# Batched matmul on one core: single buffers for the cast weights and the transposed x, x loaded ahead, casts of x between output copies

## The chip, the cores and the metric

The kernel runs on one core of a Trainium2 chip. A core has TensorE (PE, matrix products), VectorE (DVE), ScalarE (ACT), GpSimd (POOL) and SyncE (SP), which here does nothing but issue transfers. The engines run each their own list of instructions and meet only at semaphores. Data lie in HBM (the large memory), SBUF (on chip, 128 partitions) and PSUM (where TensorE writes). The metric is the device time of one launch in microseconds (us), the median of several runs.

## The reference

```python
b1, b2, m, k, n = 8, 16, 256, 512, 384
x:      (b1, b2, m, k) float32
weight: (b1, b2, k, n) float32

def reference(x, weight):
    return np.matmul(x, weight).astype(np.float32)
```

That is 128 independent products of a 256 x 512 by a 512 x 384 matrix. 67 MB of x and 101 MB of weights are read and 50 MB of results are written.

## The kernel before

The 128 products are taken in NG = 32 groups of G = 4. The 4 x 256 rows of x of a group lie in SBUF with eight rows to a partition (R = 8), so that one partition in 32 belongs to one product (C = 32). A group is worked in T = 4 steps q of two rows each. It goes through five stages:

1. SyncE (`load`, line 97) issues two transfers of weights (1.5 MB each, for two products) into `w_sb` and one of x (2 MB) into `x_sb`. Both have buffers for two groups (XS = 2 for x, WS = 4 half groups for weights). The loads run LAG = 4 groups ahead of the stores in SyncE's list, and each waits until the buffer that it fills has been cast. `store` (line 116) writes a group's result from `out_sb`, which has OS = 4 buffers.
2. ScalarE (`cast_x`, line 126) casts x to bf16 in four instructions, reordered so that two bf16 values form one 32-bit word; `x_bf` has one buffer (BS = 1).
3. TensorE (`multiply`, line 158) transposes the words of each q through an identity in four instructions, 16 per group, into four PSUM buffers `pt`.
4. VectorE (`prepare`, line 137) casts the weights of the group to bf16 in eight instructions (`w_bf`) and then, for each q, moves the transposed x out of PSUM into `x_t`. I call such a move an evacuation.
5. TensorE multiplies: for each q 32 matmuls, each with 32 columns of `x_t` as its stationary operand and 384 columns of `w_bf` moving, into one of PO = 2 PSUM buffers `po`. ScalarE (`copy_out`, line 189) copies each to `out_sb`.

The order on every engine is written out by hand, and each engine runs one loop of its own. All waits are counts on a few semaphores: `x_cast` and `w_cast` count casts, `t_made` and `t_copied` transposed steps and evacuations, `p_made` and `o_copied` multiplied and copied steps. They start at BIAS = 8 where a wait looks back. `x_in`, `w_in` and `o_out` count transfers.

Before the change `w_bf` has 2G = 8 buffers and `x_t` has TS = 2, enough for two groups. So `prepare` for group n only needs that group n-2 is multiplied (`p_made` at n*T + BIAS - T): VectorE casts the weights of n+1 while TensorE multiplies n. On ScalarE the four casts of a group stand ahead of its four copies, and on TensorE the transposes of a group ahead of its matmuls. TensorE's loop takes two groups per turn[...]; the loops of VectorE and ScalarE take two and four groups per turn.

## Time and profile before

| what | value |
|---|---|
| median of 3 runs | 518.21 us (518.1 to 518.22) |
| the profiled execution's own time | 518.98 us |
| its span | 517.2 us |
| VectorE busy | 332.8 us (64%) |
| TensorE busy with matmuls | 306.6 us (59%) |
| ScalarE busy | 236.7 us (46%) |
| mean granted TensorE clock | 0.803 |

The span is the time from the first to the last instruction of the profiled execution; its own time has what lies around the span in it. Busy times of the engines overlap and don't add up to the span. A group of instructions in the profile is named by line, engine, operation and tiles (output <- input), its form (partitions x elements and type), the count, the busy time, the mean duration of one in ns, and the idle time of the engine ahead of it with what ended most of that. The chain of waits goes back from the last instruction to what released each step. The granted clock is the share of full speed that TensorE's clock had.

### The profile page before, as it was taken

What the parts mean: (1) busy time and instruction counts of PE and PEld (TensorE: products, weight loads), DVE (VectorE), ACT (ScalarE), POOL (GpSimd) and SP (SyncE); (2) the same over time, 40 slices, a digit from 0 to 9 for tenths busy, and PEclk for the clock granted to TensorE, in tenths of its full rate; (3) what the DMA queues carried; (4) which work ended last, traced back from release to release, by engine and by line L of the source; (5) the groups of instructions that cost most, each with busy time, mean ns of one, the idle gap of its engine ahead of it and who ended that gap; (6) DMA issues with size and microseconds to landing.
All of it is one profiled execution on the core that took longest, in us unless ns stands there. A gap on an engine that the chain in (4) does not pass through costs nothing.

```text
span 517.2 us, 11523 instructions
## 1 busy us (share of the span) xinstructions
PE 306.6 (59%) x4608; PEld 200.6 (39%) x4608; DVE 332.8 (64%) x384; ACT 236.7 (46%) x264; POOL 0.7 (0%) x6
## 2 busy tenths in 40 slices
PE   0478776556665457645577554776446765467752
PEld 0345444334443334433344332444324443244431
DVE  3698875667556676556675566855658656676550
ACT  0465564443644436435355354454444544544441
POOL 0000000000000000000000000000000000000000
PEclk9998877878777887878777778877788877778777
DMA  8999999999999999999999999999999999999996
GB/s 340 430 423 424 424 432 426 429 428 430 432 427 427 427 428 432 429 427 430 426 431 431 426 429 430 427 432 427 427 429 429 427 433 425 430 428 430 429 428 251
DMA packets 18869, 218.18 MB, mean 422 GB/s; under 512 B 2096, under 2 KB 2096, under 8 KB 2608
## 3 DMA queue, kind: packets, MB, share of 16 engines
q1 hardware_dynamic: 18864, 218.11, 99.3%
q8 instruction: 3, 0.05, 0.0%
q14 instruction: 2, 0.02, 0.0%
HBM read 167.77 MB, written 50.33 MB: 422 GB/s over the span
## 4 chain that ended last, share of the span: by engine, by line
DMA 81%; ACT 10%; PE 4%; issue 3%; ACTq 0%; SPq 0%
DMA x_sb<-in_x_dram 81%; ACT x_bf L132 9%; PE po L180 2%; PE pt L166 1%; ACTq L130 0%; ACT out_sb L194 0%; SPq L111 0%; SPq L103 0%; ACT L132 0%; ACTq L193 0%; SPq L282 0%; SPq L55 0%
## 5 line engine op out<-in xcount | busy, mean ns | idle before, releaser
L147 DVE CAST w_bf<-w_sb 64x1536 bf16<-64x1536 f32 x256 | 244.4, 955 | 47.2 <-DMA w_sb<-in_weight_dram 38.5
L166 PE MATMUL pt<-identity,x_bf 128*128 128x128 f32 x512 | 123.7, 425 | 199.3 <-ACT x_bf L132 199.1
L180 PE MATMUL po<-w_bf,x_t 128*32 128x384 bf16 x4096 | 185.1, 342 | 1.0 <-issue 1.0
L166 PEld LDWEIGHTS pt<-identity,x_bf 128*128 128x128 f32 x512 | 91.8, 216 | 232.1 <-issue 218.3
L194 ACT COPY out_sb<-po 128x768 f32<-128x768 f32 x128 | 102.2, 798 | 147.2 <-PE po L180 147.2
L153 DVE COPY x_t<-pt 128x1024 bf16<-128x1024 bf16 x128 | 88.4, 691 | 122.3 <-PE pt L166 121.8
L132 ACT CAST x_bf<-x_sb 128x1024 bf16<-128x1024 f32 x128 | 124.4, 1042 | 80.9 <-DMA x_sb<-in_x_dram 80.8
L180 PEld LDWEIGHTS po<-w_bf,x_t 128*32 128x32 bf16 x4096 | 108.8, 101 | 73.8 <-issue 14.2
L132 ACT ACT_TABLE_LOAD x8 | 10.3, 1283 | 42.9 <-DMA x_sb<-in_x_dram 42.9
masks.py:199 POOL TENSOR_SCALAR_AFFINE_SELECT identity<-identity 128x128 f32<-128x128 f32 x1 | 0.3, 292 | 0.2 <-POOL identity L200 0.2
L200 POOL MEMSET identity<- 128x128 f32 x1 | 0.2, 204 | 0.5 <-SPq L55 0.5
L271 POOL MEMSET const-bfloat16-1.0<- 128x1 bf16 x1 | 0.1, 101 | 0.0
L271 POOL MEMSET const-uint8-127<- 128x1 uint8 x1 | 0.1, 101 | 0.0
L271 POOL MEMSET const-float32-0.0<- 128x1 f32 x1 | 0.1, 98 | 0.2 <-issue 0.2
L271 POOL MEMSET const-float32-1.0<- 128x1 f32 x1 | 0.1, 98 | 0.0
## 6 DMA issues: line engine op xcount, KB each, us to landing
w_sb<-in_weight_dram SPq DMA_DIRECT2D x64, 1536.0 KB, 27.5
x_sb<-in_x_dram SPq DMA_DIRECT2D x32, 2048.0 KB, 27.5
out_dram<-out_sb SPq DMA_DIRECT2D x31, 1536.0 KB, 30.7
out_dram<-out_sb SPq DMA_DIRECT2D x4, 384.0 KB, 5.9
```

Source lines behind the costliest of these rows:

```text
L132: e.copy(out=x_bf[s % BS][:, rows], in_=x_sb[s % XS][:, rows].rearrange("p r (q s c) -> p r s q c", s=S, c=KO),).then_inc(x_cast, 1)
L147: e.tensor_copy(out=w_bf[(s * G + d * D + a) % WBS][h * HP : (h + 1) * HP], in_=w_sb[slot][a * HP : (a + 1) * HP, h * KO : (h + 1) * KO, : ...
L153: e.tensor_copy(out=x_t[s % TS][:, 2 * q : 2 * q + 2], in_=pt[(s * T + q) % PT][:].bitcast(bf16),).then_inc(t_copied, 1)
L166: ins = e.transpose(pt[(s * T + q) % PT][:, rr, h, :], words[:, 2 * q + rr, h :: KO // 2], identity[:],)
L180: ins = e.matmul(po[(s * T + q) % PO][mine, rr, :N], x_t[s % TS][:, 2 * q + rr, ko // 2, mine, ko % 2], w_bf[(s * G + i) % WBS][:, ko, :], ...
L194: e.copy(out=out_sb[s % OS][:, 2 * q : 2 * q + 2, :], in_=po[(s * T + q) % PO][:, :, :N],).then_inc(o_copied, 1)
L200: e.memset(identity[:], 0.0).then_inc(id_done, 1)
L271: nc = _bacc.Bacc("TRN2", target_bir_lowering=False, num_devices=1)
```

## The change

- `w_bf` gets G = 4 buffers and `x_t` one: enough for one group.
- `load` issues x ahead of the two transfers of weights.
- `prepare` begins with the evacuations of q = 0 and 1, then waits until the group before is wholly multiplied (`p_made` at n*T + BIAS), casts the first product's weights (two instructions), evacuates q = 2 and 3, and casts the other three (six instructions). Each evacuation waits for its own step of the group before to be multiplied.
- ScalarE's order is: copies 0 and 1 of group n-1, the four casts of group n, copies 2 and 3 of group n-1. Group 0's casts stand ahead of the loop, and three groups and the last copies behind it.
- TensorE's loop takes one group per turn and is an ordinary loop of that engine.

```diff
-    BS, TS, WBS = 1, 2, 2 * G
+    BS, TS, WBS = 1, 1, G
...
     def load(e, t, U, s):
         n = t * U + s
+        if not isinstance(n, int) or n >= XS:
+            e.wait_ge(x_cast, n * T + (1 - XS) * T)
+        e.dma_start(
+            x_sb[s % XS][:],
+            x_rows[bass.ds(n * (G * M), G * M)].rearrange("(p r) k -> p r k", r=R),
+        ).then_inc(x_in[s % XS], 16)
         for d in range(G // D):
...
-        if not isinstance(n, int) or n >= XS:
-            e.wait_ge(x_cast, n * T + (1 - XS) * T)
-        e.dma_start(
-            x_sb[s % XS][:],
-            x_rows[bass.ds(n * (G * M), G * M)].rearrange("(p r) k -> p r k", r=R),
-        ).then_inc(x_in[s % XS], 16)
...
     def prepare(e, t, U, s):
         n = t * U + s
-        e.wait_ge(p_made, n * T + (BIAS - T))
-        for d in range(G // D):
-            slot = (s * (G // D) + d) % WS
-            e.wait_ge(
-                w_in[slot], (t * (U * G // D // WS) + s * G // D // WS) * 16 + 16
-            )
-            for a in range(D):
-                for h in range(S):
-                    e.tensor_copy(
-                        out=w_bf[(s * G + d * D + a) % WBS][h * HP : (h + 1) * HP],
-                        in_=w_sb[slot][a * HP : (a + 1) * HP, h * KO : (h + 1) * KO, :],
-                    ).then_inc(w_cast, 1)
-        for q in range(T):
+
+        def evacuate(q):
+            e.wait_ge(p_made, n * T + (q + 1 - T + BIAS))
             e.wait_ge(t_made, n * T + (q + 1 + BIAS))
             e.tensor_copy(
                 out=x_t[s % TS][:, 2 * q : 2 * q + 2],
                 in_=pt[(s * T + q) % PT][:].bitcast(bf16),
             ).then_inc(t_copied, 1)
+
+        def cast_w(d, a):
+            slot = (s * (G // D) + d) % WS
+            if a == 0:
+                e.wait_ge(
+                    w_in[slot], (t * (U * G // D // WS) + s * G // D // WS) * 16 + 16
+                )
+            for h in range(S):
+                e.tensor_copy(
+                    out=w_bf[(s * G + d * D + a) % WBS][h * HP : (h + 1) * HP],
+                    in_=w_sb[slot][a * HP : (a + 1) * HP, h * KO : (h + 1) * KO, :],
+                ).then_inc(w_cast, 1)
+
+        for q in range(T // 2):
+            evacuate(q)
+        e.wait_ge(p_made, n * T + BIAS)
+        cast_w(0, 0)
+        for q in range(T // 2, T):
+            evacuate(q)
+        cast_w(0, 1)
+        for a in range(D):
+            cast_w(1, a)
...
     def on_tensor(e):
-        U = 2
         e.sem_inc(t_made, BIAS)
         e.sem_inc(p_made, BIAS)
         e.wait_ge(id_done, 2)
-
-        pe = mybir.EngineType.PE
-        with nc.Fori(0, NG // U, engines=OrderedEngineSet([pe]), head_slot={pe: 0}) as t:
-            for s in range(U):
-                multiply(e, t, U, s)
+        with e.Fori(0, NG) as t:
+            multiply(e, t, 1, 0)
...
-        with e.Fori(0, NG // U) as t:
-            for s in range(U):
-                for q in range(T):
-                    cast_x(e, t, U, s, q)
-                for q in range(T):
-                    copy_out(e, t, U, s, q)
+        def step(t, U, s):
+            for q in range(T // 2):
+                copy_out(e, t, U, s - 1, q)
+            for q in range(T):
+                cast_x(e, t, U, s, q)
+            for q in range(T // 2, T):
+                copy_out(e, t, U, s - 1, q)
+
+        for q in range(T):
+            cast_x(e, 0, NG, 0, q)
+        rounds = (NG - 1) // U
+        with e.Fori(0, rounds) as t:
+            for s in range(1, U + 1):
+                step(t, U, s)
+        for n in range(rounds * U + 1, NG):
+            step(0, NG, n)
+        for q in range(T):
+            copy_out(e, 0, NG, NG - 1, q)
```

In the changed kernel the evacuation is on line 142, the weight cast on line 154, the transposes on line 177, the matmuls on line 191, the cast of x on line 131 and the copy of the output on line 205.

## The prediction

> **What bounds the kernel now.** I read the page first (span, queues, chain, groups), then the timeline of one group in the middle of the run, then windows of half a microsecond over the same stretch for the granted clock. From the page:

> ```profile
> span 517.2 us, 11523 instructions
> ...
> DMA packets 18869, 218.18 MB, mean 422 GB/s; under 512 B 2096, under 2 KB 2096, under 8 KB 2608
> ...
> q1 hardware_dynamic: 18864, 218.11, 99.3%
> q8 instruction: 3, 0.05, 0.0%
> q14 instruction: 2, 0.02, 0.0%
> ...
> DMA 81%; ACT 10%; PE 4%; issue 3%; ACTq 0%; SPq 0%
> ...
> L147 DVE CAST w_bf<-w_sb 64x1536 bf16<-64x1536 f32 x256 | 244.4, 955 | 47.2 <-DMA w_sb<-in_weight_dram 38.5
> L166 PE MATMUL pt<-identity,x_bf 128*128 128x128 f32 x512 | 123.7, 425 | 199.3 <-ACT x_bf L132 199.1
> L180 PE MATMUL po<-w_bf,x_t 128*32 128x384 bf16 x4096 | 185.1, 342 | 1.0 <-issue 1.0
> L194 ACT COPY out_sb<-po 128x768 f32<-128x768 f32 x128 | 102.2, 798 | 147.2 <-PE po L180 147.2
> L153 DVE COPY x_t<-pt 128x1024 bf16<-128x1024 bf16 x128 | 88.4, 691 | 122.3 <-PE pt L166 121.8
> L132 ACT CAST x_bf<-x_sb 128x1024 bf16<-128x1024 f32 x128 | 124.4, 1042 | 80.9 <-DMA x_sb<-in_x_dram 80.8
> ```

> The transfers are the bound: their queue is busy 99.3% of the span, the chain of waits is 81% DMA, and every engine waits for it in the end. A group's share is 218.11 MB / 32 = 6.82 MB; at the steady 428 GB/s of the middle slices that is 15.9 us. Everything that a group does on the engines must fit into a period of 15.9 us, or the bound moves. The sum of busy times doesn't tell that, the dependences do. The timeline (start, duration, engine):

> ```profile
> 30.86 0.74 PE L166 MATMUL pt<-identity,x_bf 128*128 128x128 f32 x4 [1.93 <-ACT x_bf L132]
> ...
> 43.24 3.96 PE L166 MATMUL pt<-identity,x_bf 128*128 128x128 f32 x16 [2.31 <-ACT x_bf L132]
> 44.08 0.69 DVE L153 COPY x_t<-pt 128x1024 bf16<-128x1024 bf16 x1 [1.02 <-PE pt L166]
> ...
> 258.69 3.89 ACT L132 CAST x_bf<-x_sb 128x1024 bf16<-128x1024 f32 x4
> 259.87 3.96 PE L166 MATMUL pt<-identity,x_bf 128*128 128x128 f32 x16 [6.94 <-ACT x_bf L132]
> 263.75 6.29 PE L180 MATMUL po<-w_bf,x_t 128*32 128x384 bf16 x128
> 264.72 7.85 DVE L147 CAST w_bf<-w_sb 64x1536 bf16<-64x1536 f32 x8 [0.16 <-DMA w_sb<-in_weight_dram]
> ```

> Here the eight weight casts of the next group (7.85 us) lie beside this group's matmuls (6.29 us): that is what two sets of w_bf buy. The windows of the same stretch (the column before the last two is the granted TensorE clock):

> ```profile
> 265.00:265.50 0.50, 0.50 (x12) 0.32 (x8) 0.50 (x1) 0.00 (x0) 0.00 (x0) 0.50 1.03 434
> 265.50:266.00 0.50, 0.50 (x20) 0.23 (x12) 0.47 (x2) 0.00 (x0) 0.00 (x0) 0.85 0.97 410
> 266.00:266.50 0.50, 0.50 (x20) 0.31 (x16) 0.50 (x1) 0.30 (x1) 0.00 (x0) 1.00 1.06 451
> ...
> 272.50:273.00 0.50, 0.00 (x0) 0.00 (x0) 0.07 (x1) 0.00 (x0) 0.00 (x0) 0.50 0.98 418
> ```

> TensorE has half its clock until 265.65, that is 5.8 us after its work began at 259.87; it ends that work at 270.04 and is back at half clock at 272.5. The matmuls of a group take 5.38 us in the groups where the clock rises before they begin, and up to 6.42 us where it rises later.

> [...] over the groups the clock rises between 3.3 us (132.66 to 135.9 in the windows) and 5.97 us (transposes from 338.11, matmuls of 6.42 us from 342.00: 3.89 + 2 x 1.04) after TensorE starts[...], and any idle stretch of 4.4 us or more is followed by a slow start. [...] the present loop is held: its body of two groups has 2 x 288 matmuls and weight loads, yet all instruction queues together moved 0.07 MB.

> **The change, part by part.**

> *One set of w_bf and x_t (WBS = G, TS = 1).* The new wait in prepare, p_made of the whole group before, puts all eight weight casts behind the last matmul of group n-1, while the matmuls of n need all eight. Nothing of the casts can now lie beside matmuls. Queued behind that wait on VectorE are the casts and the evacuations of q = 2 and 3; TensorE waits for both. So the period is a closed chain between two engines. From the end of the matmuls of n-1:
> - transposes of q = 0 to the first evacuation: 44.08 - 43.24 = 0.84 us at full clock (TensorE comes straight from matmuls, so it is warm), and 0.1 us for the turn between the two.
> - evacuations 0 and 1: 2 x 0.69, with 0.08 us of gaps (the transposes of a pair of rows take 0.74 us, hardly longer than an evacuation): 1.46.
> - two casts: 7.85 / 8 = 0.98 each, 1.96. Evacuations 2 and 3: 1.44. Six casts: 5.89.
> - the semaphore from VectorE to TensorE isn't in the trace; ScalarE to TensorE takes 0.13 (a cast ends 19.72, transposes start 19.85), so 0.13.
> Sum 11.82 us from the end of one group's matmuls to the start of the next.
> - the matmuls: 5.38 us at full clock. But TensorE has then stood idle since its four transposes (done after some 3 us), for 8 to 9 us, and begins at half clock. Half clock for X us costs X/2. [...] Groups of before cluster near 3.5, 4.6 and 5.7; I take their mean, 4.6, and so 2.3 us: 7.7 us.
> Period: 11.8 + 7.7 = 19.5 us, 3.6 over the transfers' 15.9. The bound leaves the DMA.

> *ScalarE's new order.* The casts of x for n stand between copies 1 and 2 of n-1. Copy 1 ends about 1 us after the matmuls of q = 1, so some 1.6 us before the last matmul; a cast's 1.05 us later the first transposes may go. The four casts (0.97 us apart) keep just ahead of transposes that take 0.74 to 0.95. On the path: nothing. If the x came late, copies 2 and 3 would be held with it, but po is then needed only 12 us later. Before, x_cast was on the path (1.17 us per group from x's landing to the transposes), but the path was one of transfers, so removing it wins nothing by itself. The table load, 8 times before (1.28 us each), is issued once; it was beside the transfers too: 0.

> *x first in the queue.* On SP, the load of x for m waits for the casts of m-2 (2 us into that group's period); the two weight loads wait for four and eight of the weight casts of m-2 (about 7.7 and 11.7 us into it), and store m-4 stands behind them. Each lands within two transfers' time, and is needed a full period or more later. The queue works 15.9 of 19.5 us and is never last. SP's count of issues is the same: 0. At the start x is there earlier: 2.33 us per MB (8.71 us for 1.57 MB, 17.27 for 5.24 MB) gives x at 10.0, the second weights at 17.3 as now. Casts and transposes of x to 16, the VectorE chain to 23 or, with the table load ahead of the first cast, 24.5; first matmuls done at 30.6 to 32.3, where they now end at 28.9. I take 31.5.

> *TensorE's loop over single groups, with no placed head.* 288 instructions and the waits, half the old body, so it should be held too. The turn now lies between matmuls and transposes, on the path, where before the wait for x covered it. The trace shows no uncovered turn. VectorE's turn shows no gap beyond 0.04 us[...]; from above I set 0.3 us (an estimate from a handful of register steps of the size of the 0.1 us issue pieces of the chain). I take the 0.1 counted above.

> **Sum.** First group 31.5, 31 periods of 19.5 = 604.5, and from the last matmul to the end 517.2 - 506.9 = 10.3 (last copy, its store, the closing steps; not touched): a span of 646.3. The profiled run of before took 518.98 around a span of 517.2, the median of the runs is 518.21, 1.0 over the span: 647 us.

> **Rivals.**
> - *Full clock throughout.* If matmuls after the pause ran at full clock, the period is 17.2: 29.2 + 533.2 + 10.3 + 1.0 = 574. Against it: every pause of 4.4 us or more in the trace ends at half clock. Chance 0.07.
> - *The clock never rises within a group.* 128 matmuls at half clock take 10.24 us (0.32 per four): period 22.1, 34 + 685 + 10.3 + 1 = 730. Against it: dense work of 6 us has always raised it. 0.03.
> - *The loop is fetched anew each turn.* The trace has one gap of 1.4 us at the first pass through new code (38.79, "issue"); one such per turn gives 647 + 31 x 1.4 = 690. Against it: the 0.07 MB above. 0.05.
> - *Not slower: the transfers stay the bound.* If the chain stayed under 15.9 us, the queue would still be full and its length decides. The last weights would then land at 496.6, as x does now, with four casts (3.9) and matmuls (5.4 to 7.7) behind: the same 517 to 521. It decides from a period 3.6 us shorter than mine, for which half clock would have to vanish and 1.3 us of VectorE's chain beside. For it: the queue is so full now that loads are always early. Against it: each VectorE duration is constant in the trace, with no contention to be freed. 0.05.
> - The forecast: 0.80.

> **How the numbers follow.** Likeliest 647. Its own range: [...] To 690 it takes in the fetch rival too; outside it lie the other three, 0.15, and a little of the forecast's own. About 0.2% (1 us) is what a measurement of this kernel can tell from no change. Faster 0.02, same 0.03 (both from the transfer rival), slower 0.95.

> **What would show it.** Right: DMA share near 0.8, the chain of waits mostly VectorE (L154, L142) and TensorE; matmuls of L191 waiting about 8.5 us for w_bf; groups of 7 to 8.5 us for 128 matmuls; VectorE waiting for transposes about 8.5 us a group. A period of 17.2 with matmuls of 5.4 us refutes the clock step; a gap between matmuls and transposes of over 0.3 us shows the loop; a queue still at 99% refutes the whole chain.

## The result, and the profile after

The changed kernel takes 618.59 us (median of 6 runs, 618.04 to 619.2) against 518.25 us of the kernel before in the same session: a ratio of 1.193, 95% interval 1.192 to 1.195. The forecast was 647, its range 615 to 690. It is slower, and by a chain between VectorE and TensorE, as forecast. The time is 28 us less than forecast, and what closes the chain was told only in part.

The page of the changed kernel, span, queue, chain of waits and the costliest groups:

```profile
span 616.7 us, 11621 instructions
...
DMA packets 18868, 218.14 MB, mean 354 GB/s; under 512 B 2097, under 2 KB 2097, under 8 KB 2609
...
q1 hardware_dynamic: 18864, 218.11, 92.4%
...
DVE 43%; PE 42%; issue 12%; DVEq 1%; DMA 1%; ACT 0%; SPq 0%
...
L191 PE MATMUL po<-w_bf,x_t 128*32 128x384 bf16 x4096 | 234.2, 402 | 274.2 <-DVE w_bf L154 274.2
...
L154 DVE CAST w_bf<-w_sb 64x1536 bf16<-64x1536 f32 x256 | 244.5, 955 | 8.0
L205 ACT COPY out_sb<-po 128x768 f32<-128x768 f32 x128 | 99.3, 802 | 386.7 <-PE po L191 386.7
L142 DVE COPY x_t<-pt 128x1024 bf16<-128x1024 bf16 x128 | 82.6, 687 | 268.9 <-PE pt L177 267.9
L131 ACT CAST x_bf<-x_sb 128x1024 bf16<-128x1024 f32 x128 | 124.4, 1047 | 6.2 <-DMA x_sb<-in_x_dram 6.2
L177 PE MATMUL pt<-identity,x_bf 128*128 128x128 f32 x512 | 87.7, 306 | 18.1 <-ACT x_bf L131 16.2
```

The chain was 81% DMA and is now 1%: VectorE 43, TensorE 42. The bytes are the same, and their mean rate falls from 422 to 354 GB/s. Read the idle columns as a pair: TensorE waits 274.2 us for the cast weights (L191 <- L154) and VectorE 267.9 us for the transposes (L142 <- L177). Two engines that wait for each other by turns, some 8.5 us each per group, are the mark of a closed chain. The casts themselves no longer wait for any transfer (they did for 38.5 us before).

The timeline of one and a half groups, start and duration in us (VectorE, ScalarE and TensorE, some lines left out):

```profile
303.87 7.85 PE L191 MATMUL po<-w_bf,x_t 128*32 128x384 bf16 x128 [8.60 <-DVE w_bf L154]
...
309.86 3.89 ACT L131 CAST x_bf<-x_sb 128x1024 bf16<-128x1024 f32 x4
...
311.65 2.02 PE L177 MATMUL pt<-identity,x_bf 128*128 128x128 f32 x12
312.43 1.29 DVE L142 COPY x_t<-pt 128x1024 bf16<-128x1024 bf16 x2 [8.85 <-PE pt L177]
...
313.75 1.94 DVE L154 CAST w_bf<-w_sb 64x1536 bf16<-64x1536 f32 x2
...
315.72 1.29 DVE L142 COPY x_t<-pt 128x1024 bf16<-128x1024 bf16 x2
317.04 5.89 DVE L154 CAST w_bf<-w_sb 64x1536 bf16<-64x1536 f32 x6
...
323.17 6.75 PE L191 MATMUL po<-w_bf,x_t 128*32 128x384 bf16 x128 [8.55 <-DVE w_bf L154]
```

Every link of the forecast chain stands here in a row: matmuls end at 311.72, evacuations, two casts, evacuations, six casts, and the next matmuls at 323.17. That is 11.45 us in which TensorE only transposes for 3. The matmuls take 7.85 and 6.75 us by turns; a group wholly at full clock takes 5.38 (e9 below). The windows of half a microsecond around three rises of the clock (the granted clock is the column before the last two):

```profile
308.50:309.00 0.50, 0.50 (x16) 0.24 (x8) 0.00 (x0) 0.00 (x0) 0.00 (x0) 0.58 0.78 319
309.00:309.50 0.50, 0.50 (x20) 0.35 (x16) 0.00 (x0) 0.34 (x1) 0.00 (x0) 1.00 1.01 393
325.50:326.00 0.50, 0.50 (x13) 0.23 (x8) 0.00 (x0) 0.03 (x1) 0.00 (x0) 0.52 0.91 344
326.00:326.50 0.50, 0.50 (x17) 0.35 (x13) 0.00 (x0) 0.50 (x1) 0.00 (x0) 1.00 1.07 418
...
346.00:346.50 0.50, 0.50 (x16) 0.24 (x8) 0.00 (x0) 0.00 (x0) 0.00 (x0) 0.54 1.01 295
```

A mean of 0.58 over a half microsecond that begins at 0.50 puts the first rise at 308.92, one of 0.52 the second at 325.98: 17.06 us apart. The third comes at 346.46 (0.54), another 20.48 us on. The trace has every stretch of one clock: the whole ones last 6.827 or 10.240 us in the changed kernel, and 3.413, 6.827, 10.240 and once 20.480 us in the kernel before. So the changes of the clock lie on a grid of 3.413 us in both. I call a step of this grid a window: 17.06 us are five, 20.48 six. The matmuls of all 31 groups from 40.68 us on begin at half clock. The groups alternate between 18.25 and 19.3 us, together eleven windows, without drift (matmuls begin at 303.87 and, ten groups on, at 491.60: 18.773 us a group, 5.5 windows are 18.77). So the period had fallen into step with the clock's windows. My likeliest number did not hold that, and the experiments below test it.

### The profile page after: what moved, and what is told of

It reads as the page before. It is cut to its first block, busy times and chain, and to the rows that moved or that the text cites. A ratio compares the mean times of both kernels' runs of the same rounds, so it can differ in the third digit from the quotient of the medians.

```text
span 616.7 us, 11621 instructions
## 1 busy us (share of the span) xinstructions
PE 319.8 (52%) x4608; PEld 209.3 (34%) x4608; DVE 327.0 (53%) x384; ACT 218.7 (35%) x257; POOL 0.7 (0%) x6
## 3 DMA queue, kind: packets, MB, share of 16 engines
q1 hardware_dynamic: 18864, 218.11, 92.4%
## 4 chain that ended last, share of the span: by engine, by line
DVE 43%; PE 42%; issue 12%; DVEq 1%; DMA 1%; ACT 0%; SPq 0%
PE po L191 38%; DVE w_bf L154 35%; DVE x_t L142 8%; PE pt L177 4%; DMA x_sb<-in_x_dram 1%; DVEq L141 1%; DVEq L235 0%; DVEq L161 0%; DVEq L150 0%; ACT x_bf L131 0%; ACT out_sb L205 0%; DVEq L140 0%; SPq L303 0%; SPq L54 0%
## 5 line engine op out<-in xcount | busy, mean ns | idle before, releaser
L191 PE MATMUL po<-w_bf,x_t 128*32 128x384 bf16 x4096 | 234.2, 402 | 274.2 <-DVE w_bf L154 274.2
L191 PEld LDWEIGHTS po<-w_bf,x_t 128*32 128x32 bf16 x4096 | 139.9, 116 | 362.4 <-issue 279.5
L154 DVE CAST w_bf<-w_sb 64x1536 bf16<-64x1536 f32 x256 | 244.5, 955 | 8.0
L205 ACT COPY out_sb<-po 128x768 f32<-128x768 f32 x128 | 99.3, 802 | 386.7 <-PE po L191 386.7
L142 DVE COPY x_t<-pt 128x1024 bf16<-128x1024 bf16 x128 | 82.6, 687 | 268.9 <-PE pt L177 267.9
L131 ACT CAST x_bf<-x_sb 128x1024 bf16<-128x1024 f32 x128 | 124.4, 1047 | 6.2 <-DMA x_sb<-in_x_dram 6.2
L177 PE MATMUL pt<-identity,x_bf 128*128 128x128 f32 x512 | 87.7, 306 | 18.1 <-ACT x_bf L131 16.2
L177 PEld LDWEIGHTS pt<-identity,x_bf 128*128 128x128 f32 x512 | 69.3, 208 | 40.1 <-issue 27.3
```

What stands on the lines that cost most here:

```text
L131: e.copy(out=x_bf[s % BS][:, rows], in_=x_sb[s % XS][:, rows].rearrange("p r (q s c) -> p r s q c", s=S, c=KO),).then_inc(x_cast, 1)
L142: e.tensor_copy(out=x_t[s % TS][:, 2 * q : 2 * q + 2], in_=pt[(s * T + q) % PT][:].bitcast(bf16),).then_inc(t_copied, 1)
L154: e.tensor_copy(out=w_bf[(s * G + d * D + a) % WBS][h * HP : (h + 1) * HP], in_=w_sb[slot][a * HP : (a + 1) * HP, h * KO : (h + 1) * KO, : ...
L177: ins = e.transpose(pt[(s * T + q) % PT][:, rr, h, :], words[:, 2 * q + rr, h :: KO // 2], identity[:],)
L191: ins = e.matmul(po[(s * T + q) % PO][mine, rr, :N], x_t[s % TS][:, 2 * q + rr, ko // 2, mine, ko % 2], w_bf[(s * G + i) % WBS][:, ko, :], ...
L205: e.copy(out=out_sb[s % OS][:, 2 * q : 2 * q + 2, :], in_=po[(s * T + q) % PO][:, :, :N],).then_inc(o_copied, 1)
```

## The experiments

The theory: the order of instructions closes a chain between VectorE and TensorE; the pause in it (8.6 us ahead of the matmuls) sends TensorE's clock to half, and the sum of both, 11.45 us and some 7.3 us, is the period. The first rival: the single buffers themselves cost the time, whatever the order. Others: the clock has no part in it; the new loop, the order on ScalarE or the order of loads does.

**e1: the buffers alone given back.**

```diff
-    BS, TS, WBS = 1, 1, G
+    BS, TS, WBS = 1, 2, 2 * G
...
-            e.wait_ge(p_made, n * T + (q + 1 - T + BIAS))
+            e.wait_ge(p_made, n * T + (q + 1 - 2 * T + BIAS))
...
-        e.wait_ge(p_made, n * T + BIAS)
+        e.wait_ge(p_made, n * T + (BIAS - T))
         cast_w(0, 0)
...
-        with e.Fori(0, NG) as t:
-            multiply(e, t, 1, 0)
+        U = 2
+        with e.Fori(0, NG // U) as t:
+            for s in range(U):
+                multiply(e, t, U, s)
```

> Two sets of cast weights and of x_t are given back (WBS = 2G, TS = 2, with the waits that look back two groups, and a loop of two groups on TensorE for the buffer numbers); the order of instructions on VectorE stays that of the changed kernel. If the buffers alone make the chain, the casts run beside the matmuls again and the time falls to that of before, 515 to 522 us. My theory is that the order alone closes it too: the first two evacuations of group n stand ahead of its casts, and their transposes stand behind the matmuls of n-1 on TensorE. Then nothing changes: 615 to 622 us.

Measured: 618.74 us. Nothing changes. VectorE's timeline in it:

```profile
312.55 1.29 DVE L142 COPY x_t<-pt 128x1024 bf16<-128x1024 bf16 x2 [7.72 <-PE pt L177]
313.87 1.94 DVE L154 CAST w_bf<-w_sb 64x1536 bf16<-64x1536 f32 x2
```

With a free set of w_bf in front of it VectorE still stands 7.72 us ahead of two evacuations. The casts behind them have no wait left that holds them; their place in the list does. So the order closes the chain by itself, and at its full length; what the single buffers do by themselves is seen in e3.

**e2: buffers and order given back** (`prepare` as before the change; x first, ScalarE's order and an ordinary loop of two groups on TensorE stay).

```diff
-    BS, TS, WBS = 1, 1, G
+    BS, TS, WBS = 1, 2, 2 * G
...
-        for q in range(T // 2):
-            evacuate(q)
-        e.wait_ge(p_made, n * T + BIAS)
-        cast_w(0, 0)
-        for q in range(T // 2, T):
-            evacuate(q)
-        cast_w(0, 1)
...
+        e.wait_ge(p_made, n * T + (BIAS - T))
+        for d in range(G // D):
...
+            for a in range(D):
+                for h in range(S):
...
+        for q in range(T):
+            e.wait_ge(t_made, n * T + (q + 1 + BIAS))
...
```

> Two sets and the old order of prepare (casts ahead of evacuations); x first, ScalarE's new order and an ordinary loop on TensorE stay. Theory: the casts lie beside the matmuls, the transfers bound the kernel again, 510 to 522 us. If any of the three parts that stay carried a loss of its own, the time would stay above 525.

Measured: 518.79 us, a ratio to before of 1.0007 (0.9998 to 1.0015). The page of e2, its chain and its costliest group:

```profile
DMA 80%; DVE 12%; issue 3%; PE 2%; ACT 1%; SPq 0%; DVEq 0%; ACTq 0%
...
L146 DVE CAST w_bf<-w_sb 64x1536 bf16<-64x1536 f32 x256 | 244.5, 955 | 178.4 <-DMA w_sb<-in_weight_dram 171.4
```

The casts wait for transfers again, now for weights, which come last. The other parts of the change together neither cost nor win anything where the transfers bound.

**e3: the order alone given back**, with one set of buffers.

```diff
-        for q in range(T // 2):
-            evacuate(q)
-        e.wait_ge(p_made, n * T + BIAS)
-        cast_w(0, 0)
-        for q in range(T // 2, T):
-            evacuate(q)
-        cast_w(0, 1)
...
+        e.wait_ge(p_made, n * T + BIAS)
+        for d in range(G // D):
...
+        for q in range(T):
+            e.wait_ge(t_made, n * T + (q + 1 + BIAS))
...
```

> One set of w_bf and x_t as in the changed kernel, but the old order of prepare: all eight casts as soon as the group before is multiplied, beside the transposes, and then the evacuations. From the end of the matmuls to the next ones: eight casts 7.9, one evacuation 0.7, semaphores 0.3 to 0.5, together some 9.0 instead of 11.47 us, since only q = 0 must be evacuated. With the matmuls at 5.38 + X/2 the period falls in step with five clock windows, 17.07 us: 29 + 31 x 17.07 + 4.7 + 1 = 564 us. With the mean X of the changed kernel (3.84) and no falling into step it would be 16.3: 540. If the one set of buffers costs the same whatever the order, 618.

Measured: 549.52 us, ratio 1.059 (1.058 to 1.061). So 69 of the 100 us lost come back with one set of buffers. My first number was 15 us too high, the one without falling into step 10 too low. The timeline:

```profile
312.44 2.57 PE L165 MATMUL pt<-identity,x_bf 128*128 128x128 f32 x16
312.67 7.86 DVE L146 CAST w_bf<-w_sb 64x1536 bf16<-64x1536 f32 x8 [6.73 <-PE po L179]
...
320.56 2.48 DVE L152 COPY x_t<-pt 128x1024 bf16<-128x1024 bf16 x4
321.31 8.29 PE L179 MATMUL po<-w_bf,x_t 128*32 128x384 bf16 x128 [6.30 <-DVE x_t L152]
```

The casts begin as soon as the matmuls end, beside the transposes, and only one evacuation, not four, lies ahead of the matmuls: 8.8 us instead of 11.45. VectorE stood idle for 6.73 us ahead of its casts, until the matmuls had freed `w_bf`, so the single set closes a chain of its own: against e2, which has two sets and the same order in `prepare`, it costs 31 us. Either of the two, the single set or the new order, keeps the casts from lying beside the matmuls; the new order makes the longer chain.

The 17.07 us that I expected are not held; the matmuls' durations drift up (6.65, 7.45, 7.91, 8.08, 8.23, 8.24, 8.31, 8.29 us in groups one after the other) and fall back to 6.65. The step would need matmuls of 8.27 us (17.07 less 8.8), a half-clock stretch of 5.8 us, near the longest in the kernel before, 6.05. Behind groups of 8.29 us comes one of 6.65, 1.64 less; by my estimate the clock rises a window earlier for it (3.413 / 2 = 1.71 us less).

**e4 and e9: the clock held up** by transposes of the identity in TensorE's pause, into columns of `po` that nobody reads; 38 per group in e4, 64 in e9.

```diff
+        e.wait_ge(o_copied, n * T + BIAS)
+        for j in range(38):
+            e.transpose(po[j % PO][:, (j // PO) % 2, N:], identity[:], identity[:])
         e.wait_ge(w_cast, n * (G * S) + G * S)
```

> The changed kernel with 38 more transposes of the identity per group on TensorE, in its pause (behind a wait for the copies of the group before), into the 128 columns of po that nobody reads. They take some 7 us and end before the weights are cast. Theory: with no pause the clock stays at full speed, the matmuls take 5.4 us in every group, the period is 11.47 + 5.4 = 16.9, and the time 28 + 31 x 16.9 + 4.7 + 1 = 557 us. If half clock isn't what lengthens the matmuls, or the transposes don't hold the clock up, 618 or, where they run over, more.

> As e4_warm, with 64 instead of 38 transposes of the identity. In e4 each took 0.115 us, so that they filled 4.4 us of the pause and left 3.6 us; in two of three groups the clock had fallen again. 64 take 7.4 us and leave some 0.5. If half clock is what lengthens the matmuls, all groups take 5.4 us, the period is 16.9 and the time 557 us. If it isn't, about 600 as in e4.

Measured: e4 601.31 us, e9 556.26 us. e4 missed its number, and its timeline says why:

```profile
305.55 4.37 PE L185 MATMUL po<-identity 128*128 128x128 f32 x38 [0.59 <-ACT out_sb L208]
...
313.52 5.38 PE L194 MATMUL po<-w_bf,x_t 128*32 128x384 bf16 x128 [3.60 <-DVE w_bf L154]
```

I had priced the fillers at the 0.185 us of the other transposes; they took 0.115, and a pause of 3.6 us remained. The groups of e4 go 5.38, 8.03, 6.84 us in turn. In e9 the pause is 0.76 us:

```profile
308.64 5.38 PE L194 MATMUL po<-w_bf,x_t 128*32 128x384 bf16 x128 [0.76 <-DVE w_bf L154]
...
325.48 5.38 PE L194 MATMUL po<-w_bf,x_t 128*32 128x384 bf16 x128 [0.76 <-DVE w_bf L154]
```

The mean granted clock is 0.999 (0.742 in the changed kernel), the matmuls take 5.38 us in both groups shown, and the period is 16.84 us. More work on TensorE makes the kernel 62 us faster: that is what half clock costs here, 62 of the 100 us lost if it is taken away first. The shares of order and clock aren't added, since each makes room for the other.

**e5 and e6: the chain lengthened** by one and two casts of weights into a spare tile.

```diff
+        for j in range(1):
+            e.tensor_copy(
+                out=spare[j][:HP],
+                in_=w_sb[s * (G // D) % WS][:HP, :KO, :],
+            )
         cast_w(0, 1)
```

> One more cast of weights on VectorE per group (0.98 us, into a tile that nobody reads), inside the chain from one group's matmuls to the next: 11.47 becomes 12.45 us. If the period is in step with clock windows of 3.413 us, it goes from 11/2 windows (18.77) to 6 windows (20.48): 31 x 1.71 = 53 us more, 671 us. If half clock costs the same mean as now whatever the phase, 31 x 0.98 = 30 more: 649 us.

> Two more casts per group, 1.96 us: the chain is 13.43 us. If the period is in step with the clock windows, it is still 6 windows, 20.48 us, and the time that of one cast more within a few us: 672 us. If half clock costs a constant mean, 31 x 1.96 = 61 more than the changed kernel: 680 us, and 30 more than with one cast.

Measured: e5 671.24 us, e6 673.45 us. The matmuls of two groups in a row, of e5:

```profile
308.40 8.19 PE L197 MATMUL po<-w_bf,x_t 128*32 128x384 bf16 x128 [9.66 <-DVE w_bf L155]
...
328.88 8.19 PE L197 MATMUL po<-w_bf,x_t 128*32 128x384 bf16 x128 [9.66 <-DVE w_bf L155]
```

and of e6:

```profile
311.48 7.32 PE L197 MATMUL po<-w_bf,x_t 128*32 128x384 bf16 x128 [10.26 <-DVE w_bf L155]
...
331.96 7.32 PE L197 MATMUL po<-w_bf,x_t 128*32 128x384 bf16 x128 [10.25 <-DVE w_bf L155]
```

Both have a period of 20.48 us, six windows. The first cast, 0.98 us of work, costs 53 us over the kernel, 1.7 a group; the second costs 2 us in all, since the matmuls get shorter by what the chain gets longer (8.19 to 7.32 us). With a constant price of half clock they were forecast at 649 and 680 us. The chain grew by less than 0.98 us a cast, to 12.29 and 13.16 us (20.48 less 8.19 and 7.32); worked out again from these, a constant price gives about 644 and 671. So the time of e6 alone would fit both readings. That of e5, 27 us above its 644, and the 2 us between the two fit only the falling into step, as do the equal periods.

**e7: ScalarE's old order** in the changed kernel (all four copies of n-1, then the casts of n).

```diff
-        def step(t, U, s):
...
+        with e.Fori(0, NG // U) as t:
+            for s in range(U):
+                for q in range(T):
+                    cast_x(e, t, U, s, q)
+                for q in range(T):
+                    copy_out(e, t, U, s, q)
```

> The changed kernel with ScalarE's old order: the casts of x for group n behind all four copies of n-1. The first transposes wait for the last copy (ends some 0.9 us after the matmuls) and the first cast (1.05 and 0.13): the chain grows by about 2.0 us to 13.5. In step with six clock windows, 20.48: 671 us. Without falling into step, 31 x 2.0 = 62 more: 680 us. If the place of these casts doesn't matter, 618.

Measured: 709.11 us, 91 more than the changed kernel: the place of the casts matters, and more than I gave it. The timeline:

```profile
356.78 1.28 ACT L131 ACT_TABLE_LOAD   x1
358.07 3.89 ACT L131 CAST x_bf<-x_sb 128x1024 bf16<-128x1024 f32 x4
359.25 0.74 PE L177 MATMUL pt<-identity,x_bf 128*128 128x128 f32 x4 [3.34 <-ACT x_bf L131]
```

Two things were missing in my sum. The old loop carries its table load (ACT_TABLE_LOAD, 1.28 us), one in four groups, and here nothing covers it: the first transposes of such a group wait 3.34 us, and its chain is 15.6 us. And even without it the chain is 13.8 to 14.2 us (the matmuls that end at 312.71 are followed by those at 326.67), over the 13.5 that I had expected to stay within six windows; most periods in the trace are 21 us or more. So ScalarE's new order, with its table load ahead of the loop, protects the changed kernel from a further 91 us, though in e2 it is worth nothing. How the 91 us divide between the two wasn't tested.

**e8: x loaded behind its weights** in the changed kernel (`load` as before the change).

> The changed kernel with x loaded behind its weights, as before the change. Theory: only the start moves. x of the first group lands at 17.3 instead of 8.8 us, the first matmuls begin near 30 instead of 22.2, the period of 18.77 stays: 7 to 9 us more, 625 to 628 us. If the order of loads matters in every group, more than 20 us either way.

Measured: 625.89 us, 7.3 more. The first matmuls of e8, and those of the changed kernel:

```profile
29.50 7.62 PE L191 MATMUL po<-w_bf,x_t 128*32 128x384 bf16 x128 [8.60 <-DVE w_bf L154]
...
22.19 7.04 PE L191 MATMUL po<-w_bf,x_t 128*32 128x384 bf16 x128 [8.29 <-DVE w_bf L154]
```

They begin the same 7.3 us later, and the period stays at 18.77 us (66.65 to 592.16 in 28 groups). The order of loads moves the start and nothing else.

**e10: one set of buffers, old order of `prepare`, clock held up** (e3 with 44 fillers).

> One set of buffers, the old order of prepare (e3) and 44 transposes of the identity in TensorE's pause. The chain would be 8.8 + 5.4 = 14.2 us, under the 15.9 us of the transfers: if order and half clock are the whole loss, the transfers bound again, 517 to 523 us, with one set of buffers. If the single buffers cost something besides, more: 530 to 550 us.

Measured: 522.58 us, ratio to before 1.007 (1.006 to 1.009). Its queue:

```profile
q1 hardware_dynamic: 18864, 218.11, 98.7%
```

The first eight groups follow one another every 14.1 us (matmuls from 21.08 to 119.91), which is the forecast chain; after them the transfers bound. Order and clock are nearly the whole loss; with both mended one set of buffers does almost as well as two. Of the 31 us that the single set costs in e3, 27 go with half clock. The 4 us left aren't settled: from 135 us on a group comes every 16.08 us here and every 15.93 us in e2, so they arise evenly along the run, but why isn't known.

**e11: TensorE's loop as before**, two groups a turn with `head_slot`.

```diff
-        with e.Fori(0, NG) as t:
-            multiply(e, t, 1, 0)
+        pe = mybir.EngineType.PE
+        with nc.Fori(0, NG // 2, engines=OrderedEngineSet([pe]), head_slot={pe: 0}) as t:
+            for s in range(2):
+                multiply(e, t, 2, s)
```

> The changed kernel with TensorE's loop as before: two groups per turn[...]. Theory: the turn costs nothing, 617 to 620 us. If the new loop's turn costs 0.3 us or more per group on the chain, the period moves and the time with it by 9 us or more.

Measured: 619.6 us (618.81 to 619.96), 1.0 more. The first matmuls begin at 23.29 instead of 22.19 us, which is all of it. The loop has no part in the loss.

No run beats the kernel before; e2 equals it.

## Why the prediction was right, and where it was off

- *The bound leaves the transfers for a chain between VectorE and TensorE*: right, shown by the chain of waits (1% DMA) and by e2, where the bound returns to the transfers.
- *The cause of the chain* was told only in part. The step "One set of w_bf and x_t" puts it down to the new wait of `prepare` for the whole group before. That wait does close a chain: in e3 it stands alone, and costs 31 us. But e1 takes it back, gives the second sets and gains nothing, because the order closes the chain too: evacuations 0 and 1 stand ahead of the casts on VectorE, and their transposes behind the matmuls on TensorE. The order also lengthens it, from 8.8 to 11.45 us. The prediction summed its chain along the new order without naming the order as a cause, so its number didn't suffer; it would have misled whoever had given the buffers back.
- *The chain of 11.8 us*: 11.45 measured. From the matmuls' end to the first evacuation it took 0.71 instead of 0.94 us, the first two evacuations ran back to back (1.29, not 1.46), and the second pair took 1.32, not 1.44; the semaphore to TensorE took 0.24, not 0.13.
- *Half clock, 2.3 us a group*: right in kind (e9), but its mean is 1.9. The term that was mis-sized is X, taken as the mean over the groups before, 4.6 us; it was 3.8 (4.94 and 2.74 by turns: twice what 7.85 and 6.75 exceed 5.38 by; the rises come 5.05 and 2.81 us after the start of the matmuls). A mean over groups whose starts were spread isn't the value of a chain that chooses its own phase. Falling into step was no part of the likeliest number.
- *The period of 19.5 us*: 18.80 over the run (first matmuls end at 29.2, last at 612.1, 31 groups), which makes 22 of the 30 us between the forecast span and the measured one.
- *The first group at 31.5 us*: 29.2, another 2.3 of the 30. x landed at 8.8, not 10.0, and the table load ran ahead of the wait for it.
- *The end, 10.3 us, "not touched"*: this is the step that failed in kind. It was 4.6 us, the last 5.7 of the 30. In the kernel before, a piece of the last store took 5.9 us to land (median of four), and now 2.3. When the transfers stopped being the bound, all of them landed sooner (x 9.0 us after its issue instead of 27.5), the last ones too.
- *ScalarE's order, the loads, the loop: nothing on the path*: right for the loop (e11; the instruction queues of the changed kernel moved 0.04 MB in four packets) and for the loads beyond the start (e8). ScalarE's order costs nothing as changed, but what it was set against, "removing it wins nothing", holds only under full transfers (e2); in the chain it is worth 91 us (e7).
- *The signs named*: the chain, TensorE's wait for `w_bf` (8.6 us a group) and VectorE's for the transposes (8.4) came as said. "DMA share near 0.8" did not: the queue was busy for 92.4% of the span, though its rate fell as reckoned (354 of 428 GB/s is 0.83). The packets of the same bytes took longer in sum, 570 us (0.924 x 616.7) instead of 514 (0.993 x 517.2); why wasn't looked for. That share by itself doesn't tell whether the queue is the bound; the chain of waits does.

## What to carry to other kernels

A second buffer lets work overlap only if the instruction list of the engine that fills it lets it start: ask what stands ahead of that work in its engine's list and on whose list that waits. The missing buffer and such an order can each close the chain, so giving back one of them may show nothing (e1). Compare the length of the closed chain, not busy shares, with the period of the transfers; here every engine is busy for less than two thirds of the span before and after. Where TensorE pauses in each round, as here for 8.6 us, look for a stretch at half clock (3.8 us on the mean here) and whether the rounds fall in step with the clock's changes (3.413 us apart or a multiple of that here) before a change of some tenths of a microsecond is called a gain or a loss.
